# One more step between transposes and value products in a hybrid attention and S5 layer, with S5's scans in two steps and its rotation back on GpSimd

## The chip, the cores and the metric

The kernel runs on one core of a Trainium2 chip. The metric is the device time of one execution in microseconds; the median of three runs of the kernel before is 1433.84 us (1433.35 to 1434.98). Engines are named as the profile names them: PE (matmuls) and PEld (its weight loads), DVE (VectorE), ACT (ScalarE), POOL (GpSimd), SP (the engine that issues most DMAs).

## What is computed

One encoder layer over 2048 positions of 1024 channels, in float32. A projection is split into latent attention (4 heads) and an S5 branch (32 groups of 16 channels, 64 complex states, forward and backward); both branches are normed, gated, joined and projected back. Cut to what matters here:

```
for each block of queries and each head:                       # attention
    s = qn . k_nope + qr . k_rope                              # scores
    p = softmax(s * scale);   o = p . v
bu = einsum(u, b_bar)                                          # S5, both directions
_, h = associative_scan(h_t = lam_bar * h_(t-1) + bu_t)
y  = Re(einsum(h, c)) + d_skip * u
```

## The kernel before

The kernel writes out the order of every engine by hand: each engine executes its instructions in the order in which the code issues them (`manual_schedule`), and an instruction that waits holds up all that stand behind it on its engine. There are three stages. The first projects the input. The second, in which the change lies, is attention with S5 between its pieces. The third mixes, projects back and stores.

**The attention stage** is a loop over steps `t` (L1547). A unit is 256 queries of one head; there are 32 units of 8 steps, so 256 steps with scores. In step `t`:

- `scores` (L1098): five matmuls of 512 columns into a PSUM tile `sc` (two buffers), then DVE takes the negative maximum `nm` (L1108).
- `expo` (L1111): ACT writes `e = exp(sc + nm)` (L1114) into a ring of 13 tiles. Nine steps later `norm` scales it on ACT (L1143).
- `transp` (L1145), 11 steps after the exponential (`LAG`): four PE transposes of two `e` tiles into PSUM `pt` (two buffers); ACT rounds them to `phi` (L1159) and DVE stores the rest `plo = pt - phi` (L1573). Both have two buffers.
- `av` (L1163), `AVLAG` = 1 step after the transposes: six matmuls that read `phi` and `plo` (L1171 to L1173) and add into `av` in PSUM (one buffer). After a unit's eighth `av`, ACT copies the sum to `avs` (L1176), and one step later `unit_out` multiplies it by a weight into `po` (L1180), which ACT copies to `o` (L1182).
- Pieces of `qprep` (L703) make the queries of the next block of four units: 19 pieces, in the steps that a rule allows (steps 4 of a unit are left out, step 3 only ends a piece). They use the PSUM pool `psQ`, which has one buffer. `unit_out` uses the same buffer, in step 4 of a unit.

**S5 between them.** A group of channels (`group`, L950) starts every 7 steps (twice after 6), and takes 15 steps, so two groups are always under way. "pre" pieces stand ahead of a step's scores, "post" pieces behind its value products. Counted from the group's start: steps 0 to 3 make tables on POOL (`w`, `tmp`, `t`, `t3b`; L905 to L975), step 3 turns `w` on PE, step 5 makes `px` on PE, step 6 multiplies it by phasors on DVE (`ta`, `tb`, L996 and L997), step 7 adds them to `X` (L1001), step 8 scans them in four scans on DVE (L1008 and L1009, two for each of the real and imaginary parts, into `G`), step 9 turns them back (`hc` on DVE at L1017, `tb` on POOL at L1018), step 10 subtracts (L1021, DVE), and step 14 multiplies `hc` into `py` on PE (L1034). Other POOL work of the stage: tables `v` of the next four groups, splits `ul` and `ml`, and `qd` of the queries (L750).

The loop's end, as it matters here:

```
        # (without scores in between, its operands take a step longer)
        lag = AVLAG + (t >= 8 * NU)
        m, j = divmod(t - LAG - lag, 8)
        if 0 <= m < NU and t != 8 * NU:
            av(sts[m], j)
        m, j = divmod(t - LAG - lag - 1, 8)
        if 0 <= m < NU and j == 7:
            unit_out(*units[m], sts.pop(m))
        s5_post(t)
```

Of the kernel before, what the change touches and what calls it, by code (L numbers as in the profile page):

```python
# [21 lines left out]
P = 128  # L22
# [11 lines left out]
T = 8  # L34
# [22 lines left out]
class Metered:  # L57
    """An engine that counts the elements it is given."""
# [13 lines left out]
class Scratch:  # L72
    """Temporaries of one shape, out of a ring of tiles of 512 (or, if small, 32) elements."""
# [10 lines left out]
def reduce_angle(eng, sc, out, ang):  # L84
    """out = ang - 2 pi round(ang / 2 pi)."""
    k = sc()
    eng.tensor_scalar(k, ang, 1.0 / TWO_PI, MAGIC, ALU.mult, ALU.add)
    eng.tensor_scalar(k, k, MAGIC, None, ALU.subtract)
    yield
    eng.scalar_tensor_tensor(out, k, -PI_1, ang, ALU.mult, ALU.add)  # L90
    for c in (PI_2, PI_3, PI_4):
        yield
        eng.scalar_tensor_tensor(out, k, -c, out, ALU.mult, ALU.add)
    yield


def sincos(eng, sc, sin_out, cos_out, r):
    """sin and cos of r in about [-pi, pi], from those of r / 2."""
# [23 lines left out]
def exp_of(eng, sc, pool, out, x):  # L122
    """exp(x) in float32, exact at 0."""
# [24 lines left out]
def tile_hymba(ctx, tc, x, pos, inv_freq, pre_g, w_in, q_g, w_uqT, w_uqr, kv_g, w_ukT, w_uv, attn_g,  # L148
# [35 lines left out]
    def rsqrt_of(ss, n, scale, eps=EPS):  # L184
        """(ss * scale + eps) ** -0.5 on [128, n]."""
        v = sm.tile([P, n], F32, tag=f"rv{n}", name="rv")
        r = sm.tile([P, n], F32, tag=f"rr{n}", name="rr")
        V.tensor_scalar(v, ss, scale, eps, ALU.mult, ALU.add)
        G.tensor_tensor(r, v, nhalf[:, :n], ALU.pow)
        return r  # L190

    def split(hi, lo, src, scale=None):
        """hi + lo = src (* a scale for each partition), both float32r."""
        if scale is None:
            A.activation(hi, src, AF.Copy)
            V.tensor_tensor(lo, src, f32(hi), ALU.subtract)
        else:
            A.activation(hi, src, AF.Copy, scale=scale)
            V.scalar_tensor_tensor(lo, src, scale, f32(hi), ALU.mult, ALU.subtract)
# [6 lines left out]
    # tables of the attention phase; those of S5 go through DRAM, by groups  # L206
# [11 lines left out]
    # ------------------------------------------------------------------ phase 1  # L218
# [51 lines left out]
    def turn(xt, t):  # L270
        """The tile's transpose, split, as tile t of a pair."""
# [34 lines left out]
    def gemm_t(nm, half):  # L306
        """Two blocks of 128 columns of a pair of tiles, with the columns in the partitions."""
# [43 lines left out]
    def s5_params():  # L351
# [37 lines left out]
        # F = (lam_bar - 1) / lam  # L389
# [17 lines left out]
        # powers of lam_bar, 0 .. T, in the order of each direction  # L407
# [29 lines left out]
        # phasors of chunk 32 i + 2 j + a: ph32 * (0..7) (+ phi), for a = 0, 1, and ph2 * (0..15)  # L437
# [13 lines left out]
        for nm, src in (("b", ph2), ("a", ph32)):  # L451
# [21 lines left out]
            # the backward direction turns the other way  # L473
# [11 lines left out]
        # B_bar = F B; B'' = B_bar e^{-i phi}; C' = lam_bar C  # L485
# [3 lines left out]
        def cm(orr, oi, ar, ai, xr_, xi_):  # L489
            """(orr, oi) = (ar + i ai)(xr + i xi), a over the last dimension."""  # L490
# [32 lines left out]
        # centre lag: Re(C B_bar) of both directions + D  # L523
        # (eight groups at a time: theirs are the blocks on the diagonal)
# [36 lines left out]
    def step():  # L561
        """A slice of the tables, of about BUDGET elements."""
# [4 lines left out]
    def blocks(s):  # L567
        """The columns of two tiles, a block of columns at a time: z goes first and last, tile by tile,
        so that the next tiles can take the places of these meanwhile."""
# [8 lines left out]
    # absorbed weights: W_uq[h] W_uk[h]^T  # L578
# [23 lines left out]
    # the first tile is loaded and normed by halves  # L602
# [48 lines left out]
    # ------------------------------------------------------------------ phase 2  # L651
    # (the gate columns of the last two tiles run under its start)
# [5 lines left out]
    ep = pool(ph2, "ep", 13)  # L658
    pp = pool(ph2, "pp", 2)
# [36 lines left out]
    # queries of a block of 256: each piece's last results are split a step later  # L696
# [74 lines left out]
    def both(*gens):  # L771
        """Step some routines in turn; what each returns."""
# [14 lines left out]
    # the gate columns of the last two tiles run under the start of the attention  # L787
# [58 lines left out]
    # S5  # L846
# [8 lines left out]
    def s5_load(q):  # L855
        """The tables of four groups."""
# [34 lines left out]
    def ops4(tile_, q_r, q_i, c1, c2):  # L891
        """The operands of tile_[., 2, s, h] = q_r[s] c1[., h] + q_i[s] c2[., h]."""
# [9 lines left out]
    def two(eng, tile_, tmp, *o):  # L902
        """The two products of a table; later they are added."""
# [18 lines left out]
    def k_build(q):  # L922
        """The kernels of the lags within a chunk, and their windows for each position."""
# [26 lines left out]
    def group(g):  # L950
        """A group of channels, a step at a time: what is ready first, what needs the PE last."""
        q, i = divmod(g, 4)
        f = S5[q]
        # (chunks in the order of their tiles: those of the even, then those of the odd places)
# [9 lines left out]
        # phasors over the chunks: -sin, cos, sin  # L964
# [39 lines left out]
        # (the states that enter the chunks; nothing enters the first, or the last backwards)  # L1004
# [6 lines left out]
        yield "pre"  # L1011
        yield "post"
# [4 lines left out]
        V.tensor_tensor(of_tiles(hc), g4, co, ALU.mult)  # L1017
# [3 lines left out]
        V.tensor_tensor(hc, hc, tb2, ALU.subtract)  # L1021
        yield "pre"
        yield "post"
# [20 lines left out]
    # when each group starts; the tables of the next four groups are made meanwhile  # L1044
# [52 lines left out]
    # attention  # L1097
# [19 lines left out]
    # the blocks of a row were shifted by their own maxima: bring them to the row's, and divide  # L1117
# [45 lines left out]
    def av(st, j):  # L1163
# [10 lines left out]
        if j == 7:  # L1174
            st["avs"] = op.tile([P, 256], F32, tag="avs", name="avs")
# [9 lines left out]
    # ------------------------------------------------------------------ weights of phase 3  # L1185
# [52 lines left out]
    # ------------------------------------------------------------------ phase 3  # L1238
    # (pairs of tiles, with the channels in the partitions up to W_out)
    def mixer():  # L1240
# [26 lines left out]
        def gelu(d):  # L1267
            """y <- 2 gelu(y), and its parts"""
# [38 lines left out]
        def part(d, src, h, c):  # L1307
            """hi and lo of half h of src, as blocks c .. of the products' operands"""
# [16 lines left out]
        def summed(d, sq):  # L1325
            """The sums of squares of the four channels in a partition"""
# [5 lines left out]
        def attn(d):  # L1332
            """o gated, and its parts"""
# [16 lines left out]
        def ssm(d):  # L1350
            """y <- 4 y sigmoid(. + b), gated into g, and its parts"""
# [37 lines left out]
        # the columns of the result in the parts that are worked on; the last tile ends in smaller ones  # L1389
# [11 lines left out]
        def comb(d, t, cs):  # L1401
            """Both branches by their factors, summed; the mean of the squares; times the gain"""
# [40 lines left out]
        # the first pairs, in small steps between those of the attention  # L1443
# [98 lines left out]
    NLAG, LAG, AVLAG = 9, 11, 1  # L1542
# [4 lines left out]
    for t in range(8 * NU + LAG + AVLAG + 3):  # L1547
        n, i = divmod(t, 8)
        # what the step before has made ready
# [5 lines left out]
        # scores  # L1555
# [23 lines left out]
        # (without scores in between, its operands take a step longer)  # L1579
        lag = AVLAG + (t >= 8 * NU)  # L1580
        m, j = divmod(t - LAG - lag, 8)
        if 0 <= m < NU and t != 8 * NU:
            av(sts[m], j)
        m, j = divmod(t - LAG - lag - 1, 8)
# [3 lines left out]
        # the queries of the next block  # L1588
# [37 lines left out]
def layout(i):  # L1626
    """The inputs, laid out for the core; nothing is computed from them."""
# [51 lines left out]
```

## Time and profile before

| | before |
|---|---|
| time, median of 3 runs | 1433.84 us (1433.35 to 1434.98) |
| span of the profiled execution | 1431.5 us |
| PE busy | 1359.6 us, 95% |
| PEld busy | 1221.6 us, 85% |
| DVE busy | 1053.7 us, 74% |
| ACT busy | 789.0 us, 55% |
| POOL busy | 624.9 us, 44% |

The span runs from the first to the last instruction of the one profiled execution; the time of the runs holds 2.3 us more. PE's busy time counts matmuls whose ends are modelled, so a busy PE is not PE at its peak. The 256 steps of the attention stage lie between about 394 and 1168 us of the span.

### The profile page before, as it was taken

How to read it: one execution, taken by the hardware profiler on the slowest of the kernel's cores; microseconds unless marked ns; L12 is line 12 of the kernel's file. 1: busy time of each engine (PE TensorE's matmuls, PEld its weight loads, DVE VectorE, ACT ScalarE, POOL GpSimd, SP SyncE). 2: the span in 40 equal slices, each digit the busy share in tenths (PEclk: the TensorE clock that was granted, in tenths of full speed). 3: DMA queues.
4: the chain of work that ended last, by engine and by line, in shares of the span. 5: the costliest groups of instructions: out<-in, count | busy, mean ns of one | idle time of the engine just before them, and what ended most of it. 6: DMA issues, size and time to landing. Idle time of an engine off the chain costs nothing.

```text
span 1431.5 us, 24291 instructions
## 1 busy us (share of the span) xinstructions
PE 1359.6 (95%) x9016; PEld 1221.6 (85%) x9016; DVE 1053.7 (74%) x1876; ACT 789.0 (55%) x1796; POOL 624.9 (44%) x616
## 2 busy tenths in 40 slices
PE   7999999999989999999999998999999989999998
PEld 7999999999968788887888887887888878788886
DVE  5456545332588888898989888988888895876774
ACT  6321222122457767767677676676677775544542
POOL 2102321233364655555556555645542695323340
PEclk9999999999999999999999999999999999999999
DMA  8322332442610110201102011020100345345432
GB/s 293 89 61 66 80 87 73 98 122 73 150 35 19 39 34 5 54 19 31 41 5 61 12 32 41 23 43 5 32 5 9 101 128 131 118 148 179 145 103 88
DMA packets 122133, 102.91 MB, mean 72 GB/s; under 512 B 14672, under 2 KB 107104, under 8 KB 122016
## 3 DMA queue, kind: packets, MB, share of 16 engines
q1 hardware_dynamic: 110384, 89.43, 22.3%
q0 software_dynamic: 2272, 7.62, 2.0%
q10 hardware_dynamic: 9360, 4.33, 1.5%
q8 instruction: 70, 1.15, 0.3%
q14 instruction: 47, 0.39, 0.1%
HBM read 63.80 MB, written 37.54 MB: 71 GB/s over the span
## 4 chain that ended last, share of the span: by engine, by line
PE 59%; DVE 26%; ACT 5%; issue 4%; POOL 2%; DMA 2%; SPq 1%; ACTq 0%; POOLq 0%; DVEq 0%
DVE plo L1573 5%; DVE nm L1108 4%; PE po L202 4%; PE po L203 4%; PE po L204 4%; PE pt L1151 3%; DVE hc L1017 3%; DVE G L1009 3%; DVE G L1008 3%; PE z_ga L203 2%; PE z_ga L204 2%; PE z_ga L202 2%; PE av L1173 2%; PE z_u L204 2%; PE z_u L202 2%
## 5 line engine op out<-in xcount | busy, mean ns | idle before, releaser
L1114 ACT ACTIVATE e<-sc,nm 128x512 f32<-128x512 f32 x256 | 176.4, 689 | 141.1 <-DVE nm L1108 139.8
L1573 DVE TENSOR_TENSOR plo<-pt,phi 128x512 fp32r<-128x512 f32 x255 | 175.0, 686 | 49.2 <-ACT phi L1159 46.3
L1159 ACT ACTIVATE phi<-pt 128x512 fp32r<-128x512 f32 x256 | 152.8, 597 | 72.9 <-PE pt L1151 72.4
L1108 DVE TENSOR_REDUCE nm<-sc 128x1 f32<-128x512 f32 x256 | 175.0, 683 | 17.6 <-PE sc L1107 15.6
L1173 PE MATMUL av<-plo,kn_h 128*128 128x256 f32 x512 | 150.6, 294 | 30.0 <-DVE plo L1573 29.5
L1171 PE MATMUL av<-phi,kn_h 128*128 128x256 f32 x512 | 165.7, 324 | 13.3 <-ACT avs L1176 13.2
L1143 ACT ACTIVATE e<-e,f 128x512 f32<-128x512 f32 x226 | 163.8, 725 | 1.5 <-DVE f L1132 1.5
L1151 PEld LDWEIGHTS pt<-ident,e 128*128 128x128 f32 x1024 | 127.8, 141 | 38.9 <-DVE e L1139 4.5
L1151 PE MATMUL pt<-ident,e 128*128 128x128 f32 x1024 | 154.8, 274 | 4.3 <-DVE e L1139 3.5
L1172 PE MATMUL av<-phi,kn_l 128*128 128x256 f32 x512 | 144.6, 282 | 0.0
L1173 PEld LDWEIGHTS av<-plo,kn_h 128*128 128x128 f32 x512 | 96.5, 189 | 40.1 <-DVE plo L1573 39.3
L1018 POOL TENSOR_TENSOR tb<-G,t 128x512 f32<-128x512 f32 x32 | 41.6, 1301 | 192.2 <-DVE G L1009 192.2
L1103 PE MATMUL sc<-kT_h,qo 128*128 128x512 f32 x256 | 114.7, 448 | 2.9 <-ACT e L1114 1.4
L1171 PEld LDWEIGHTS av<-phi,kn_h 128*128 128x128 f32 x512 | 97.6, 191 | 16.6 <-ACT avs L1176 16.5
L202 PE MATMUL po<-woh,ah 128*128 128x512 f32 (+1 forms) x264 | 102.6, 389 | 1.9 <-ACT u L1410 1.9
L203 PE MATMUL po<-wol,ah 128*128 128x512 f32 (+1 forms) x264 | 102.4, 388 | 0.0
L204 PE MATMUL po<-woh,al 128*128 128x512 f32 (+1 forms) x264 | 102.3, 388 | 0.0
L1104 PE MATMUL sc<-kT_l,qo 128*128 128x512 f32 x256 | 101.5, 396 | 0.0
L1106 PE MATMUL sc<-krS,qo 128*128 128x512 f32 x256 | 101.3, 396 | 0.0
L1107 PE MATMUL sc<-krS,qo 128*128 128x512 f32 x256 | 101.2, 395 | 0.0
L1105 PE MATMUL sc<-kT_h,qo 128*128 128x512 f32 x256 | 100.8, 394 | 0.0
L1172 PEld LDWEIGHTS av<-phi,kn_l 128*128 128x128 f32 x512 | 97.7, 191 | 0.0
(337 smaller groups left out, 4148.6 us busy)
## 6 DMA issues: line engine op xcount, KB each, us to landing
g_d<-gst SPq DMA_DIRECT2D x64, 128.0 KB, 2.0
g<-g_d SPq DMA_DIRECT2D x16, 512.0 KB, 5.7
xr<-in_x_dram SPq DMA_DIRECT2D x16, 512.0 KB, 6.7
xt<-in_x_dram SPq DMA_DIRECT2D x15, 512.0 KB, 3.8
out_dram<-res SPq DMA_DIRECT2D x15, 512.0 KB, 3.1
u_d<-ust ACTq DMA_DIRECT2D x64, 64.0 KB, 2.1
u<-u_d SPq DMA_DIRECT2D x64, 64.0 KB, 2.5
o_d<-o SPq DMA_DIRECT2D x32, 128.0 KB, 1.8
```

What stands on the lines that cost most here:

```text
L202: PE.matmul(ps, ahi, bhi, start=first, stop=False)
L203: PE.matmul(ps, ahi, blo, start=False, stop=False)
L204: PE.matmul(ps, alo, bhi, start=False, stop=last)
L1108: V.tensor_reduce(st["nm"][:, qt, kb:kb + 1], ps, AX.X, ALU.max, negate=True)
L1114: A.activation(e, st.pop("s"), AF.Exp, bias=st["nm"][:, qt, kb:kb + 1], accum_out=st["L"][:, qt, kb:kb + 1])
L1143: A.activation(e, e, AF.Copy, scale=f)
L1151: PE.transpose(pt[:, kk, qt, :], st["e"][qt, kt // 4][:, o:o + P], ident)
L1159: A.activation(hi, ptf, AF.Copy)
L1171: PE.matmul(o, kn_h[:, kt, :], hi[:, w], start=kt == 0, stop=False)
L1172: PE.matmul(o, kn_l[:, kt, :], hi[:, w], start=False, stop=False)
L1173: PE.matmul(o, kn_h[:, kt, :], lo[:, w], start=False, stop=kt == NT - 1)
L1573: V.tensor_tensor(lo[0], lo[1], f32(lo[2]), ALU.subtract)
```

## The change

The value products follow two steps behind the transposes (`AVLAG` 1 to 2), `phi` and `plo` get three buffers, the ring of `e` goes from 13 tiles to 12 and `avs` from two to one. The lag behind the last scores was two steps before and still is, so the special case there goes. S5's four scans are spread over two steps, the real part's two in step 8 and the imaginary part's two in step 9. The rotation back moves a step, to 10 and 11, and its DVE product (L1017) and its subtraction (L1021) go to POOL. `py` stays in step 14. Comments are blanked too, and lines below the loop's special case stand two to four lines higher.

```diff
-    ep = pool(ph2, "ep", 13)
-    pp = pool(ph2, "pp", 2)
+    ep = pool(ph2, "ep", 12)
+    pp = pool(ph2, "pp", 3)
...
         for r in range(2):
             o = r * NC
             V.tensor_tensor_scan(gt[0:64, o + 2:o + NC + 1], df[0:64], xm[0:64, r, 0:NC - 1], 0.0, ALU.mult, ALU.add)
             V.tensor_tensor_scan(gt[64:P, o + 1:o + NC][:, ::-1], df[64:P], xm[64:P, r, 1:][:, ::-1], 0.0,
                                  ALU.mult, ALU.add)
-        yield "pre"
-        yield "post"
+            yield "pre"
+            yield "post"
...
-        V.tensor_tensor(of_tiles(hc), g4, co, ALU.mult)
+        G.tensor_tensor(of_tiles(hc), g4, co, ALU.mult)
         G.tensor_tensor(of_tiles(tb2), g4[:, ::-1], si, ALU.mult)
         yield "pre"
         yield "post"
-        V.tensor_tensor(hc, hc, tb2, ALU.subtract)
-        yield "pre"
-        yield "post"
+        G.tensor_tensor(hc, hc, tb2, ALU.subtract)
...
-            st["avs"] = op.tile([P, 256], F32, tag="avs", name="avs")
+            st["avs"] = op.tile([P, 256], F32, tag="avs", name="avs", bufs=1)
...
-    NLAG, LAG, AVLAG = 9, 11, 1
+    NLAG, LAG, AVLAG = 9, 11, 2
...
-    for t in range(8 * NU + LAG + AVLAG + 3):
+    for t in range(8 * NU + LAG + AVLAG + 2):
...
-        lag = AVLAG + (t >= 8 * NU)
-        m, j = divmod(t - LAG - lag, 8)
-        if 0 <= m < NU and t != 8 * NU:
+        m, j = divmod(t - LAG - AVLAG, 8)
+        if 0 <= m < NU:
             av(sts[m], j)
-        m, j = divmod(t - LAG - lag - 1, 8)
+        m, j = divmod(t - LAG - AVLAG - 1, 8)
```

The built order of the instructions shows three places. The first is DVE's queue where a group is scanned and turned back. `nm` and `plo` are the attention's two DVE instructions of a step, and the scans print as SCALAR_TENSOR_TENSOR. Before:

```order
L1008 SCALAR_TENSOR_TENSOR G_4637<-tab_6803,X_4639 64x255
L1009 SCALAR_TENSOR_TENSOR G_4637<-tab_6803,X_4639 64x255
L1008 SCALAR_TENSOR_TENSOR G_4637<-tab_6803,X_4639 64x255
L1009 SCALAR_TENSOR_TENSOR G_4637<-tab_6803,X_4639 64x255
L1108 TENSOR_REDUCE nm<-sc 128x1
L1573 TENSOR_TENSOR plo<-pt_8811,phi 128x512
L1017 TENSOR_TENSOR hc<-G_4637,t_8563 128x512
L1108 TENSOR_REDUCE nm<-sc 128x1
L1573 TENSOR_TENSOR plo<-pt_8853,phi 128x512
L732 SCALAR_TENSOR_TENSOR qo_1_8828<-psq,kvgs,qo_1_8828 128x256
L1021 TENSOR_TENSOR hc<-hc,tb_8839 128x512
```

The same group in the changed kernel:

```order
L1008 SCALAR_TENSOR_TENSOR G_4637<-tab_6797,X_4639 64x255
L1009 SCALAR_TENSOR_TENSOR G_4637<-tab_6797,X_4639 64x255
L1106 TENSOR_REDUCE nm<-sc 128x1
L1571 TENSOR_TENSOR plo<-pt_8797,phi 128x512
L1008 SCALAR_TENSOR_TENSOR G_4637<-tab_6797,X_4639 64x255
L1009 SCALAR_TENSOR_TENSOR G_4637<-tab_6797,X_4639 64x255
L1106 TENSOR_REDUCE nm<-sc 128x1
L1571 TENSOR_TENSOR plo<-pt_8843,phi 128x512
L732 SCALAR_TENSOR_TENSOR qo_1_8820<-psq,kvgs,qo_1_8820 128x256
L1106 TENSOR_REDUCE nm<-sc 128x1
```

Two scans stand between one step's `plo` and the next step's `nm`, where four stood, and the two `hc` instructions are gone from DVE.

The second place is POOL's queue from one group's turn back to the next group's tables (`t`, `t3b`: phasor tables of the next group; `w`, `v`: tables of later ones; `G` are the scanned states). Before:

```order
L1018 TENSOR_TENSOR tb_8036<-G_4638,t_7745 128x512
L971 TENSOR_TENSOR t_8039<-tab_6803 128x768
L972 TENSOR_TENSOR t3b<-tab_6803 128x768
L975 TENSOR_TENSOR t_8039<-t_8039,t3b 128x768
L905 TENSOR_TENSOR v<-tab_7930 128x256
L906 TENSOR_TENSOR tmp<-tab_7930 128x256
L915 TENSOR_TENSOR v<-v,tmp 128x256
```

In the changed kernel:

```order
L971 TENSOR_TENSOR t_8029<-tab_6797 128x768
L972 TENSOR_TENSOR t3b<-tab_6797 128x768
L1017 TENSOR_TENSOR hc<-G_4638,t_7735 128x512
L1018 TENSOR_TENSOR tb_8059<-G_4638,t_7735 128x512
L975 TENSOR_TENSOR t_8029<-t_8029,t3b 128x768
L1021 TENSOR_TENSOR hc<-hc,tb_8059 128x512
L905 TENSOR_TENSOR v<-tab_7924 128x256
L906 TENSOR_TENSOR tmp<-tab_7924 128x256
L915 TENSOR_TENSOR v<-v,tmp 128x256
```

POOL now waits for the scans behind the next group's `t` and `t3b`, not ahead of them, and carries two more instructions of 512 elements in each group.

The third place is PE's queue around `unit_out` (`po`) and a piece of the queries (`ptr`, four transposes of `qd`), which both write the one buffer of `psQ`. Before, `po` stands a step earlier, at the end of the step of `pt_6544`, and the queries' piece at the end of this one:

```order
L1151 MATMUL pt_6583<-ident,e 128x128 x4
L1171 MATMUL av<-phi,kn_h 128x256
L1172 MATMUL av<-phi,kn_l 128x256
L1173 MATMUL av<-plo,kn_h 128x256
L1171 MATMUL av<-phi,kn_h 128x256
L1172 MATMUL av<-phi,kn_l 128x256
L1173 MATMUL av<-plo,kn_h 128x256
L758 MATMUL ptr_6600<-ident,qd 128x128 x4
L1103 MATMUL sc<-kT_h,qo_2_5050 128x512
```

In the changed kernel:

```order
L1149 MATMUL pt_6569<-ident,e 128x128 x4
L1169 MATMUL av<-phi,kn_h 128x256
L1170 MATMUL av<-phi,kn_l 128x256
L1171 MATMUL av<-plo,kn_h 128x256
L1169 MATMUL av<-phi,kn_h 128x256
L1170 MATMUL av<-phi,kn_l 128x256
L1171 MATMUL av<-plo,kn_h 128x256
L1178 MATMUL po<-avs,wuv 128x256
L758 MATMUL ptr_6592<-ident,qd 128x128 x4
L1101 MATMUL sc<-kT_h,qo_2_5044 128x512
```

`po` has moved from step 4 of a unit to step 5, in which the queries' rule lets a piece begin: the piece follows it in the same step. In the whole order a piece of the queries follows `po` in its step 17 times, before never; six of these have S5 matmuls between the two (three times `py` from `hc`, three times `py` and `px`).

## Rows read from the trace of the kernel before

**Rows 1.** The page's part 1: busy us, share of the span, instructions.

```profile
PE 1359.6 (95%) x9016; PEld 1221.6 (85%) x9016; DVE 1053.7 (74%) x1876; ACT 789.0 (55%) x1796; POOL 624.9 (44%) x616
```

**Rows 2.** Busy time by stage; columns: stretch, us, five engines, granted clock, DMA share, GB/s.

```profile
0.00:394.20 394.20, 383.81 (x2929) 374.41 (x2929) 193.89 (x460) 117.99 (x256) 93.39 (x130) 1.00 0.40 108
394.20:1167.90 773.70, 725.30 (x4713) 632.86 (x4714) 679.84 (x1163) 543.66 (x1273) 429.87 (x400) 1.00 0.14 33
1167.90:1431.50 263.60, 250.49 (x1377) 214.29 (x1375) 179.93 (x256) 127.34 (x268) 101.63 (x87) 0.99 0.43 131
```

**Rows 3.** Waits of PE in 394.2 to 1167.9: us in total, times, longest.

```profile
PE av L1173 <- DVE plo L1573: 29.1, 34, 2.6
PE av L1171 <- ACT avs L1176: 12.8, 11, 1.8
```

**Rows 4.** Waits of PE's weight loads in the same stretch, same columns.

```profile
PEld av L1173 <- DVE plo L1573: 38.7, 44, 2.8
PEld av L1171 <- ACT avs L1176: 15.8, 13, 2.0
```

**Rows 5.** The chain that ended last, around one step: start us, us, what.

```profile
739.60 0.23 PE sc L1103
...
740.76 0.44 PE pt L1151 x4
...
741.90 0.12 PE py L202
...
742.25 0.12 PE px L202
...
742.97 0.23 PE sc L1103
```

**Rows 6.** Groups of DVE in the stage: busy us, mean ns, then idle before them.

```profile
L1108 DVE TENSOR_REDUCE nm<-sc 128x1 f32<-128x512 f32 x255 | 174.3, 683 | 17.6 <-PE sc L1107 15.6
L1573 DVE TENSOR_TENSOR plo<-pt,phi 128x512 fp32r<-128x512 f32 x243 | 166.8, 686 | 45.1 <-ACT phi L1159 42.1
L1017 DVE TENSOR_TENSOR hc<-G,t 128x512 f32<-128x512 f32 x32 | 52.3, 1635 | 0.0
L1009 DVE TENSOR_TENSOR_SCAN G<-tab,X 64x255 f32<-64x255 f32 x64 | 46.3, 724 | 0.9
...
L1021 DVE TENSOR_TENSOR hc<-hc,tb 128x512 f32<-128x512 f32 x32 | 41.3, 1292 | 2.5 <-POOL tb L1018 2.5
L1001 DVE TENSOR_TENSOR X<-ta,tb 128x512 f32<-128x512 f32 x32 | 23.8, 743 | 0.0
```

**Rows 7.** DVE in order of time behind one group's scans: start us, us.

```profile
730.03 0.69 DVE L1573 TENSOR_TENSOR plo<-pt,phi 128x512 fp32r<-128x512 f32 x1
730.63 2.02 DVE L1017 TENSOR_TENSOR hc<-G,t 128x512 f32<-128x512 f32 x1
```

**Rows 8.** POOL in the same stretch.

```profile
729.35 1.30 POOL L1018 TENSOR_TENSOR tb<-G,t 128x512 f32<-128x512 f32 x1 [4.59 <-DVE G L1009]
730.61 1.50 POOL L971 TENSOR_TENSOR t<-tab 128x768 f32<-128x768 f32 x1
```

**Rows 9.** Groups of POOL in the stage: busy us, mean ns, idle before.

```profile
L975 POOL TENSOR_TENSOR t<-t,t3b 128x768 f32<-128x768 f32 x32 | 63.1, 1971 | 2.2
...
L1018 POOL TENSOR_TENSOR tb<-G,t 128x512 f32<-128x512 f32 x32 | 41.6, 1301 | 192.2 <-DVE G L1009 192.2
```

**Rows 10.** All engines around one `unit_out`, in order of time.

```profile
701.70 0.59 PE L1180 MATMUL po<-avs,wuv 128*128 128x256 f32 x2
...
701.94 0.58 PE L1103 MATMUL sc<-kT_h,qo 128*128 128x512 f32 x1
...
702.40 0.39 ACT L1182 ACTIVATE o<-po 128x256 f32<-128x256 f32 x1
...
704.44 1.03 PE L1034 MATMUL py<-hc,v 128*128 128x256 f32 x4
...
705.12 0.47 PE L202 MATMUL psr<-wqr_h,zh 128*128 128x256 f32 x1
```

## The prediction

> **What bounds the kernel now.** I read the busy times first, then the same by stage, then the waits of PE and of its weight loads, then the chain of waits around single steps, and last the groups and the order in time of the engines that PE waits for. PE is busy 95% of the span [rows 1], but that is an average of three stages. In the first stage PE misses 10 us of 394 and in the third 13 of 264; in the attention stage it misses 48 of 774, at the full granted clock, 1.00, the level of 2.4 GHz [rows 2]. The change touches only that stage, so what it can give is what PE loses there.
>
> The waits name the loss. PE stands idle 29.1 us before products that read `plo`, which DVE makes, and 12.8 us before the first product of a unit, which needs the `avs` copy of the unit before to be done [rows 3]. The weight loads, which run ahead of the matmuls and so show a stop earlier, wait 38.7 and 15.8 us for the same two [rows 4]. The reader is to see that both views put nearly all of the loss on these two places: 41.9 us by the matmuls, whose modelled ends cover the beginning of each wait, and 54.5 us by the loads. I take 54.5 us as what can be won at most from waits that are named.
>
> That it is a loss and not work shows in a step without a wait. In the chain the five score matmuls start at 739.60, the transposes at 740.76, and after the products S5's matmuls at 741.90: 2.30 us for the attention's part. S5's nine matmuls take it to 742.97, 1.07 us more [rows 5]. The stage has 255 steps from the first scores to the last in 773.7 us [rows 2], so 3.03 us a step on average; without 54.5 us of waits it would be 2.82 us.
>
> DVE is why `plo` is late. It is busy 679.84 us of the stage [rows 2], 2.67 us a step, against a PE that could run at 2.82; that is near enough to fall behind wherever the work is bunched. `hc` and its subtraction take 1635 and 1292 ns on average, while `X`, an addition of the same size from SBUF to SBUF, takes 743 and `plo` 686 [rows 6]. The order in time shows why: `hc` begins at 730.63, as POOL begins `t` at 730.61, and ends at 732.65, 0.54 us after POOL's instruction has [rows 7, 8]. So an instruction of DVE with both operands in SBUF stands still while POOL runs one, and `plo`, one operand of which is in PSUM, does not: 0.69 us at 730.03, while POOL runs from 729.35 to 730.65. In a group four scans of 724 ns [rows 6], and one step later the long `hc` and the long subtraction, all stand ahead of some step's `plo`; PE can't pass, since its next products read it.
>
> **The change part by part.**
>
> *The products a step later.* `plo` may be one step late, 2.8 us, before PE waits for it. The longest wait of PE for `plo` is 2.8 us, and 38.7 us over 44 waits is 0.9 us each [rows 4], so the slack alone covers nearly all of them. But it removes no work from DVE, and PE then runs into the next limits: scores need an `sc` buffer that the exponential of two steps before has freed, which needs that step's `nm` from the same DVE. Alone, I would expect a good part of 38.7 us to come back at `sc`. The three buffers of `phi` and `plo` keep a step's ACT and DVE work from waiting for products two steps back. The shorter ring of `e` costs nothing: tile `t - 12` was last read by the transposes of step `t` or earlier, and ACT's `phi` of step `t`, which stands ahead of the exponential, waits for these anyway. One `avs` is enough, since it is read a step after it is written and rewritten eight steps later.
>
> *DVE without `hc`.* 52.3 + 41.3 = 93.6 us leave DVE [rows 6]: 586 us remain, 2.30 us a step against PE's 2.82. This cures the cause, and is hidden by nothing: it is what makes `nm` come in time, for `sc` and for `avs` too, whose copy stands on ACT behind an exponential that waits for `nm`.
>
> *The scans in two steps.* A scan step held 2.8 us of scans and 1.4 us of `nm` and `plo`, above any step of PE's; now two steps hold 1.4 + 1.4 = 2.8 us each, which is about PE's step. The heaviest DVE steps are now even.
>
> *POOL with `hc`.* The product should cost what its twin `tb` costs, 1301 ns. For the subtraction I have the addition of 768 elements, 1971 ns, so 1.31 us for 512, between 1.30 and 1.97 as bounds [rows 9]. 32 x 2.61 = 84 us more: POOL goes from 429.87 [rows 2] to 514 us in a stage of some 735, 70%. What hides it is POOL's idle time, 192.2 us of which are spent waiting for the scans [rows 9]. The result is needed in step 14 and is begun in step 10: POOL has four steps, 11 us, for `hc`, `tb`, the `t` addition and the subtraction, 1.3 + 1.3 + 2.0 + 1.3 = 5.9 us. If that cover is gone, PE waits for `hc` at `py`. The next group's `t` and `t3b` come out of the wait for the scans, which is easier for them.
>
> *DVE against POOL.* The instructions that still read SBUF twice on DVE are `X`, the scans and the small ones of the row statistics. They stand late in the 7 steps, when POOL has mostly gone through its queue. POOL's load becomes 514/32 = 16 us of a group's 20 (7 x 2.82), so `X` will meet it at times. A meeting costs what `hc` paid, 2.02 - 0.68 = 1.34 us with `plo` for the bare cost [rows 7]. I take one meeting a group, 1.34 x 32 = 43 us of DVE, which DVE has: 629 us, 2.47 a step. The Trainium skill says of this in SBUF — State Buffer, "Who interferes with whom", that only DVE's and GpSimd's shared ports contend, and that whoever holds them holds them for a whole instruction. The trace agrees (2.02 us beside 0.69). By that rule each of the five instructions of a group would meet POOL as often as POOL is busy, 0.7, and wait half a meeting, 0.67 us: 75 us of DVE in the stage in place of 43. DVE would then hold 661 us, 2.59 a step, still under PE's, and the sum stays.
>
> *The new meeting in `psQ`.* `po` now stands in step 5 of a unit, in which a queries' piece may follow at once; both want the one buffer, and the rule still keeps step 4 free. 17 times the piece must wait until ACT has copied `po`. Before, PE had issued `po` by 701.94 and ACT's copy ended at 702.79: 0.85 us [rows 10]. Eleven bare cases cost 9.4 us; three with `py` between (704.44 to 705.12, 0.68 us [rows 10]) 0.5 us; three with nine matmuls (1.07 us [rows 5]) nothing. 9.9 us together, and between nothing (PE late anyway) and 17 x 1.7 = 29 (a copy that a late exponential holds up as long again).
>
> **The sum.** 54.5 us of named waits, less 9.9 for `psQ`, 4 that stay of the wait for `plo` (a tenth), and 5 of the wait for `avs` (a third: one buffer of `av` remains, and the copy still stands behind an exponential) gives 35.6. The profiled execution had a span of 1431.5 us and the runs' median lies 2.3 above it, so 1395.9 + 2.3, about 1398 us.
>
> **Rivals.**
>
> *The wait moves.* PE runs into `sc` and into ACT. ACT is busy 543.66 us of the stage [rows 2], 2.13 a step, and works in order; a short PE step of 2.30 us leaves it little room. Then `avs` keeps all of its 15.8, the `plo` waits come back by half as waits for the exponential, 19, and `psQ` takes 9.9: 54.5 - 44.7 = 10 us won, 1424. For it: after the change no engine between PE and PSUM has gained a buffer but `phi`. Against: DVE's 93.6 us are gone, and the present waits of PE for the exponential are small enough not to be among the first two.
>
> *POOL holds DVE.* This ends on the other side. If POOL's queue has not run out when the next group's `X` and scans come, each of the five waits 1.34 us: 6.7 us a group, where the removed two cost 2.9. DVE then has 586/32 = 18.3 + 6.7 = 25.0 us a group, against 773.7/32 = 24.2 now (the stage's last steps counted in): 0.8 x 32 = 26 us slower, 1460. It decides from 5.9 us a group, more than four of the five held. For it: POOL's load of 16 us nearly fills the time from the second pair of scans to the next first pair, 20 - 2.8 - 1.4 = 15.8. Against: the load counts work that is spread, such as `qd` and the weights at the end. The Trainium skill speaks for it in Perfetto Trace Analysis, "Optimizing Scalar/DVE Operations": since the two engines share a port of SBUF, moving work from the one to the other might not help. The trace agrees so far as `hc` paid 1635 ns.
>
> *It does nothing.* If the waits in the trace were only PE's spare time before another limit, all 54.5 us would come back, 1434. Against: the limit would have to be PE itself, and PE does a step in 2.30.
>
> **Chances.** My forecast 0.80, the moved wait 0.12, POOL holding DVE 0.05, nothing 0.03. The predicted time is the likeliest, 1398. Its own range runs from 1379 (all 54.5 us won and `psQ` free) to 1417 (`psQ` at 29 us); the range given, 1380 to 1420, reaches toward the moved wait and leaves out the far part of it. A measurement of this kernel tells 0.2%, 3 us, from no change: faster 0.91, within 0.2% 0.03, slower 0.06.
>
> **What the profile after would show.** The wait of the products for `plo` gone, and DVE's busy time in the stage near 590 to 630 us. `hc` and the subtraction on POOL at about 1.3 us each. Scans and `X` still near 0.7 us; above 1.2 us the second rival is at work. A new wait of PE's query matmuls for ACT's `o`, some 10 us. If the named waits of PE for the exponential or `avs` grow above 20 us, the first rival holds. The first and third stages should keep their 394 and 264 us. The prediction is wrong if POOL sits idle little and `py` waits for it, or if PE's short steps turn out to be paced by ACT.

## The result and the profile after

The changed kernel takes 1411.2 us (median of 4 runs, 1410.1 to 1413.6), the kernel before 1433.6 beside it: ratio 0.9844, 95% interval 0.983 to 0.9858. It is 22.4 us faster; 35.6 were forecast. 1411 lies inside the range given, 1380 to 1420, but in its slower half.

The stages of the changed kernel, with the columns of [rows 2]:

```profile
0.00:393.70 393.70, 384.38 (x2929) 374.91 (x2929) 193.54 (x460) 117.69 (x256) 93.35 (x130) 1.00 0.40 109
393.70:1143.20 749.50, 715.82 (x4707) 626.93 (x4708) 620.80 (x1099) 546.40 (x1273) 497.82 (x464) 1.00 0.14 34
1143.20:1408.30 265.10, 252.84 (x1383) 216.25 (x1382) 179.71 (x255) 127.01 (x268) 101.09 (x87) 0.99 0.43 130
```

The attention stage is 24.2 us shorter, 749.5 for 773.7, and the third stage 1.5 us longer. DVE's busy time in the stage fell by 59 us and POOL's rose by 68. The waits of PE's weight loads in the stage, which answer to [rows 4]:

```profile
PEld sc L1101 <- ACT e L1112: 16.6, 19, 2.7
PEld ptr L758 <- ACT o L1180: 8.1, 5, 3.1
PEld av L1169 <- ACT avs L1174: 7.8, 10, 1.8
PEld psq L202 <- ACT o L1180: 6.3, 4, 2.6
PEld psr L202 <- ACT o L1180: 1.9, 2, 0.9
```

In the kernel before, the score matmuls waited for the exponential as well, a little:

```profile
PEld sc L1103 <- ACT e L1114: 3.6, 6, 1.2
```

The wait for `plo` is gone and that for `avs` halved. In their place stand 16.6 us of score matmuls that wait for the exponential, and 16.3 us in three rows of queries' matmuls that wait for ACT's `o`: the meeting in `psQ`. These named waits come to 40.7 us; before, the waits for `plo`, for `avs` and of the scores came to 58.1.

DVE's groups in the stage, as in [rows 6], and POOL's two new ones, as in [rows 9]:

```profile
L1009 DVE TENSOR_TENSOR_SCAN G<-tab,X 64x255 f32<-64x255 f32 x64 | 57.1, 892 | 0.9
L1008 DVE TENSOR_TENSOR_SCAN G<-tab,X 64x255 f32<-64x255 f32 x64 | 51.8, 810 | 0.0
L1001 DVE TENSOR_TENSOR X<-ta,tb 128x512 f32<-128x512 f32 x32 | 30.8, 963 | 0.0
...
L1017 POOL TENSOR_TENSOR hc<-G,t 128x512 f32<-128x512 f32 x32 | 41.6, 1300 | 134.8 <-DVE G L1009 106.4 <-PE pt L1149 12.3 <-PE av L1171 10.7
L1021 POOL TENSOR_TENSOR hc<-hc,tb 128x512 f32<-128x512 f32 x32 | 41.4, 1292 | 0.6
```

`hc` and the subtraction cost on POOL what was forecast, 83 us. POOL's other instructions took 15 us less than before; that DVE's two had held them in their turn would fit, and is not tested. The scan of L1009 has gone from 724 to 892 ns and `X` from 743 to 963: they are now the ones that POOL holds. One group's scans and `X` on DVE show it:

```profile
860.93 1.98 DVE L1001 TENSOR_TENSOR X<-ta,tb 128x512 f32<-128x512 f32 x1
...
864.83 2.16 DVE L1009 TENSOR_TENSOR_SCAN G<-tab,X 64x255 f32<-64x255 f32 x1
```

POOL in the same stretch:

```profile
860.87 1.50 POOL L971 TENSOR_TENSOR t<-tab 128x768 f32<-128x768 f32 x1
862.32 1.95 POOL L972 TENSOR_TENSOR t3b<-tab 128x768 f32<-128x768 f32 x1
864.35 2.09 POOL L975 TENSOR_TENSOR t<-t,t3b 128x768 f32<-128x768 f32 x1
```

`X` began 0.06 us after `t` and ended at 862.91, 0.54 us behind it; the scan ended at 866.99, 0.55 us behind the addition. POOL is held in its turn: `t3b` began at 862.32, while `X` was still at work, and took 1.95 us where `t`, of the same size, took 1.50. What holds the scans and `X` are mostly the tables of the next group, which in the kernel before POOL reached only after these scans: in the trace of the stage, 22 of the 31 us by which scans and `X` exceed their undisturbed time (139.7 us for 108.7) fall on instructions that met `t`, `t3b` or their addition.

The longest meeting in `psQ`, PE, ACT and the DMA that ACT waited for, in order of time:

```profile
838.03 0.59 PE L1178 MATMUL po<-avs,wuv 128*128 128x256 f32 x2
839.24 0.63 ACT L887 ACTIVATE mh<-m 128x512 fp32r<-128x512 f32 x1 [2.66 <-DMA m<-k_d]
839.78 0.58 ACT L1157 ACTIVATE phi<-pt 128x512 fp32r<-128x512 f32 x1
...
840.25 0.68 ACT L1112 ACTIVATE e<-sc,nm 128x512 f32<-128x512 f32 x1
...
840.92 0.38 ACT L1180 ACTIVATE o<-po 128x256 f32<-128x256 f32 x1
...
841.35 0.65 PE L758 MATMUL ptr<-ident,qd 128*128 128x128 f32 x4 [2.73 <-ACT o L1180]
```

`po` was on its way at 838.03 and its copy came at 840.92, since `phi`, the exponential and, here, a split that waited for its DMA stand ahead of it on ACT. All of PE's later work stood behind the four transposes of the queries until 841.35.

### The profile page after: what moved, and what is told of

Its sections match the earlier page's. It is cut to its first block, busy times and chain, and to the rows that moved or that the text cites. A ratio compares the mean times of both kernels' runs of the same rounds, so it can differ in the third digit from the quotient of the medians.

```text
span 1408.3 us, 24276 instructions
## 1 busy us (share of the span) xinstructions
PE 1353.0 (96%) x9016; PEld 1218.1 (86%) x9016; DVE 994.0 (71%) x1812; ACT 791.1 (56%) x1796; POOL 692.3 (49%) x680
## 4 chain that ended last, share of the span: by engine, by line
PE 70%; DVE 16%; ACT 6%; issue 3%; POOL 2%; DMA 1%; SPq 1%; POOLq 0%; ACTq 0%; DVEq 0%
PE pt L1149 5%; PE po L202 4%; PE po L204 4%; PE po L203 4%; DVE nm L1106 3%; PE sc L1101 3%; DVE G L1009 2%; PE sc L1102 2%; PE sc L1105 2%; PE sc L1104 2%; PE sc L1103 2%; PE av L1169 2%; PE av L1170 2%; PE av L1171 2%; PE z_ga L203 2%
## 5 line engine op out<-in xcount | busy, mean ns | idle before, releaser
L1106 DVE TENSOR_REDUCE nm<-sc 128x1 f32<-128x512 f32 x256 | 175.4, 685 | 45.5 <-PE sc L1105 42.7
L1171 PE MATMUL av<-plo,kn_h 128*128 128x256 f32 x512 | 144.4, 282 | 0.4 <-DVE plo L1571 0.4
L1017 POOL TENSOR_TENSOR hc<-G,t 128x512 f32<-128x512 f32 x32 | 41.6, 1300 | 134.8 <-DVE G L1009 106.4
L189 POOL TENSOR_TENSOR rr<-rv,nhalf 128x1 f32<-128x1 f32 (+1 forms) x23 | 17.0, 741 | 163.7 <-DVE rv L188 163.7
```

What stands on the lines that cost most here:

```text
L1106: V.tensor_reduce(st["nm"][:, qt, kb:kb + 1], ps, AX.X, ALU.max, negate=True)
L1171: PE.matmul(o, kn_h[:, kt, :], lo[:, w], start=False, stop=kt == NT - 1)
```

## The experiments

Each was timed against the kernel before on the same chip. "The moved rule" below is the edit of the third.

**The two halves of the change, and its S5 half by parts.** `e1_lag_only` takes only the attention's part of the diff:

```diff
-    NLAG, LAG, AVLAG = 9, 11, 1
+    NLAG, LAG, AVLAG = 9, 11, 2
```

with the buffers and the loop's end as in the change.

> Only the attention part of the change: products two steps behind the transposes, three buffers of both parts, 12 tiles of e, one avs; S5 as before, with hc and its subtraction on DVE. Theory (DVE's lateness is the cause, the lag only moves the wait): the wait of the products for plo goes, 38.7 us by the weight loads, and most of it comes back as waits of the score matmuls for the exponential and of the first products for avs, 25 us or more together; psQ adds its meeting; time 1420 to 1432 us. Rival (the lag is the gain, DVE's work was only in the way of plo): waits for the exponential stay under 10 us and the time is about that of the changed kernel, 1405 to 1415 us.

Measured: 1453.2 us, ratio 1.0137 (1.0114 to 1.0161), slower than either theory had it. The weight loads' waits:

```profile
PEld sc L1103 <- ACT e L1114: 31.3, 35, 3.1
PEld av L1171 <- ACT avs L1176: 21.1, 17, 2.5
PEld ptr L758 <- ACT o L1182: 8.9, 5, 2.3
PEld psq L202 <- ACT o L1182: 7.5, 4, 2.5
PEld psr L202 <- ACT o L1182: 3.7, 4, 1.4
```

The wait for `plo` is gone. In its place stand 31.3 us at the scores, where 3.6 stood, and 5.3 more at `avs`; 20.1 us of `psQ` come on top. There is a price that I had not counted, the clock. Eight stretches of 2 us of this run, columns as in [rows 2]:

```profile
622.00:624.00 2.00, 1.67 (x13) 1.34 (x12) 2.00 (x4) 1.45 (x4) 1.92 (x2) 1.00 0.00 0
624.00:626.00 2.00, 1.25 (x8) 0.83 (x6) 2.00 (x2) 0.43 (x1) 1.94 (x3) 1.00 0.00 0
626.00:628.00 2.00, 0.52 (x4) 0.52 (x5) 1.21 (x3) 1.62 (x5) 1.84 (x4) 1.00 0.00 0
628.00:630.00 2.00, 1.38 (x7) 0.66 (x6) 1.45 (x3) 1.84 (x5) 1.92 (x4) 0.59 0.03 8
630.00:632.00 2.00, 2.00 (x8) 1.90 (x9) 0.00 (x0) 0.42 (x2) 0.28 (x1) 0.50 0.23 66
632.00:634.00 2.00, 2.00 (x7) 1.51 (x7) 0.28 (x1) 0.66 (x2) 0.00 (x0) 0.50 0.00 0
634.00:636.00 2.00, 2.00 (x14) 2.00 (x13) 1.15 (x3) 1.37 (x4) 0.00 (x0) 0.70 0.00 0
636.00:638.00 2.00, 2.00 (x15) 1.74 (x14) 1.58 (x4) 0.51 (x1) 0.00 (x0) 1.00 0.00 0
```

PE, the first of the five busy times, falls to 0.52 us of 2, and the granted clock then goes to 0.50, the level of 1.2 GHz, while PE is fully busy; it is back at 1.00 in the last row. Over the whole run the granted clock is 0.991, against 0.997 before: by an estimate from these two, 0.006 x 1447 = 9 us. The attention stage of this execution is 16.1 us longer than before (789.8 for 773.7): PE is idle 9.8 us more and busy 6.3 us more (731.6 for 725.3). Slower matmuls would show in the second of these, so the estimate looks somewhat high.

`e2_s5_only` is the other half, S5's part of the diff on the kernel before, with the lag of one.

> Only the S5 part of the change: scans in two steps, rotation back on GpSimd; products one step behind the transposes as before, two buffers, 13 tiles of e. Theory (DVE's 93.6 us are the cause): the wait for plo falls from 38.7 us by the weight loads to under 20 without any lag, there is no meeting in psQ, and the time is 1408 to 1420 us. Rival (the lag is the gain): plo keeps over 30 us of waits and the time stays above 1425 us.

Measured: 1402.5 us, ratio 0.9787 (0.9772 to 0.9801), below the theory's range, though `plo` keeps 22.3 us of waits, a little more than it said. The rival falls, and the half is faster than the whole.

`e11_hc_pool_only` takes only two lines of it:

```diff
-        V.tensor_tensor(of_tiles(hc), g4, co, ALU.mult)
+        G.tensor_tensor(of_tiles(hc), g4, co, ALU.mult)
...
-        V.tensor_tensor(hc, hc, tb2, ALU.subtract)
+        G.tensor_tensor(hc, hc, tb2, ALU.subtract)
```

> The kernel before with nothing changed but the engine of hc and its subtraction, GpSimd in place of DVE: lag of one, scans in one step, rotation in steps 9 and 10. Theory (this move alone is the gain): 1398 to 1408 us, with waits for plo of 15 to 28 us by the weight loads. Rival (without spreading or lag the four scans ahead of a step's plo keep PE waiting): 1415 us or more.

Measured: 1400.2 us, ratio 0.9766 (0.9751 to 0.9781). The weight loads' waits for what PE waited for before:

```profile
PEld av L1173 <- DVE plo L1573: 18.4, 26, 2.9
PEld av L1171 <- ACT avs L1176: 5.4, 7, 1.7
```

So 33 us come from two instructions moved to another engine, with no lag and no spreading: the wait for `plo` halves and that for `avs` falls to a third. The intervals of this kernel and of the S5 half overlap: spreading the scans with the rotation a step later, as the change does it, gave nothing.

`e5_hc_dve` is the opposite, the changed kernel with those two lines back on DVE.

> The changed kernel with the rotation back on VectorE again (hc and its subtraction), in its new steps 10 and 11; scans still in two steps, products still two steps behind. Theory (it is hc and the subtraction on DVE, held by GpSimd, that make DVE late): DVE's busy time in the stage rises from 621 to 670 us or more, waits for the exponential and avs rise by 10 us or more, and the time is 1418 to 1428 us. Rival (the bunch of four scans was the cause, and spreading them is enough): the time stays within 4 us of the changed kernel's 1411.

Measured: 1443.5 us, ratio 1.0078 (1.0058 to 1.0098), 16 us above the theory's range: waits for the exponential 24.5, for `avs` 21.7 and for `o` 20.3 us, and a granted clock of 0.990. The rival falls: the two lines are worth 32 us in the changed kernel too.

**The meeting in `psQ`.** `e3_rule` is the changed kernel with the queries' rule moved on by a step, as `po` was:

```diff
-            if qb and (held if i == 3 else i != 4 and PLACE.get(t, (0, 0))[1] in QOFF):
+            if qb and (held if i == 4 else i != 5 and PLACE.get(t, (0, 0))[1] in QOFF):
```

> The changed kernel with the queries' rule moved on by a step, as po has moved: step 5 of a unit is left out in place of step 4, and step 4 only ends a piece in place of step 3, so no piece follows po in its step. Theory (the meeting in psQ costs what the waits for ACT's o show, 11.8 us by the matmuls and 16.3 by the weight loads): those waits go and the time falls by 9 to 16 us, to 1395 to 1402 us. Rival (while PE waits for o, DVE and ACT catch up, so the waits come back at the scores): the time falls by under 4 us, and the waits of the scores for the exponential rise from 16.6 us to over 25.

Measured: 1397.4 us, ratio 0.9747 (0.9732 to 0.9761), 13.8 us under the changed kernel. The waits for `o` are down to 0.6 us, and what is left is:

```profile
PEld sc L1101 <- ACT e L1112: 12.6, 19, 2.5
PEld av L1169 <- ACT avs L1174: 11.0, 13, 2.3
```

The rise at `avs`, 3 us, is all that came back; the theory holds. Against `e2_s5_only`, which lacks only the lag, its buffers and the moved rule, this kernel is 5 us faster.

`e6_lag_rule` is the kernel of `e1_lag_only` with the moved rule.

> The kernel before with the lag of two and its buffers, and with the queries' rule moved on by a step so that no piece follows po; S5 as before. Theory (the lag by itself gives next to nothing while DVE is late, and the 20 us by which the lag alone was slower are the meeting in psQ, 20.1 us of waits by the weight loads, with the clock dips that follow it): time 1428 to 1438 us, as the kernel before. Rival (the lag itself is harmful, since PE runs ahead into the one buffer of av and the two of sc): 1442 us or more. Second rival (the lag is a gain once psQ is free): 1422 us or less.

Measured: 1429.2 us, ratio 0.9969 (0.9958 to 0.9981). With `psQ` free the lag alone gives 4 us and no more: 28.3 us of waits for the exponential and 19.5 for `avs` stand where 38.7 for `plo` and 15.8 for `avs` stood. The theory holds; the meeting turned a small gain into a loss of 20 us.

**The scans and the order of POOL's queue.** `e7_rule_one_scan` has the moved rule, and all scans in step 8 with the rotation on POOL in steps 9 and 10, the places of the kernel before.

> The changed kernel with the moved queries' rule, and S5's four scans in one step again; hc and its subtraction stay on GpSimd, one step earlier, py where it is. Theory (what counts is the amount of work on DVE and GpSimd's holding of it, not the bunching): within 4 us of the 1397 us of the same kernel with scans in two steps. Rival (the spreading of the scans is a large part of the gain): 1403 us or more, with waits of the scores for the exponential 8 us or more above the 12.6 us there.

Measured: 1394.0 us, ratio 0.9716 (0.97 to 0.9732), the fastest kernel of the study, with 13.7 us of waits for the exponential: the theory holds, bunching the scans again costs nothing here. It differs from `e11_hc_pool_only` in the lag, its buffers and the moved rule alone, and the intervals of the two lie apart (0.97 to 0.9732, 0.9751 to 0.9781): with DVE relieved and `psQ` free, the lag is worth 6 us. `e10_rule_one_scan_hc_late` differs from `e7_rule_one_scan` in one thing: the rotation stands a step later, in 10 and 11, as the change has it.

```diff
+        yield "pre"
+        yield "post"
         g3 = gt[:, 1:2 * NC + 1].rearrange("p (a c) -> p a c", a=2)
...
         G.tensor_tensor(hc, hc, tb2, ALU.subtract)
-        yield "pre"
-        yield "post"
```

> The changed kernel with the moved queries' rule, all four scans in step 8, and the rotation back in steps 10 and 11 as in the changed kernel, so that GpSimd's queue has the next group's t and t3b ahead of its wait for the scans. Theory (in the changed kernel the order of GpSimd's queue sets t and t3b against the scans on DVE, and what spreading the scans gives is given back by that): scans and X are held by 20 us or more in all, as with the scans in two steps (32 us) and unlike the 9 us with the rotation in steps 9 and 10, and the time is 1397 to 1406 us. Rival (GpSimd's order does not matter, the scans are simply better bunched): 1391 to 1396 us, as with the rotation in steps 9 and 10.

Measured: 1419.1 us, ratio 0.9898 (0.988 to 0.9916): 25 us slower than the kernel that it differs from by this step, more than the theory said. DVE's scans and `X` in `e7_rule_one_scan`:

```profile
L1009 DVE TENSOR_TENSOR_SCAN G<-tab,X 64x255 f32<-64x255 f32 x64 | 47.1, 736 | 0.9
L1008 DVE TENSOR_TENSOR_SCAN G<-tab,X 64x255 f32<-64x255 f32 x64 | 46.1, 721 | 0.4
L1001 DVE TENSOR_TENSOR X<-ta,tb 128x512 f32<-128x512 f32 x32 | 24.1, 752 | 0.0
```

and in `e10_rule_one_scan_hc_late`:

```profile
L1009 DVE TENSOR_TENSOR_SCAN G<-tab,X 64x255 f32<-64x255 f32 x64 | 60.7, 948 | 0.9
L1008 DVE TENSOR_TENSOR_SCAN G<-tab,X 64x255 f32<-64x255 f32 x64 | 56.0, 874 | 0.4
L1001 DVE TENSOR_TENSOR X<-ta,tb 128x512 f32<-128x512 f32 x32 | 28.1, 880 | 0.0
```

The later wait lets POOL run the next group's `t` and `t3b` against the scans, and the scans and `X` are held 27.5 us more. In the traces 29 us of this kernel's holding fall on instructions that met `t`, `t3b` or their addition, and 1 us of that of `e7_rule_one_scan`. The waits of the scores for the exponential are 29.0 us for 13.7, and the granted clock is 0.991 for 0.998, 10 us of 1420.

`e13_spread_forward` spreads the scans the other way, without that step: the first two behind `X` in step 7, the others in step 8, the rotation in 9 and 10.

> The changed kernel with the moved queries' rule and the scans spread the other way: the real part's two in step 7 behind X, the imaginary part's two in step 8, and the rotation on GpSimd in steps 9 and 10, so that GpSimd waits for the scans ahead of the next group's t and t3b, as in the kernel before. Theory (spreading the scans helps, and in the changed kernel GpSimd's order gave it back): X and the scans are held under 12 us in all, and the time is 1380 to 1391 us, under the 1394 us of the scans in one step with the same order. Rival (with GpSimd's order kept, bunched scans cost nothing more): 1392 us or more.

Measured: 1395.1 us, ratio 0.974 (0.9724 to 0.9756). It is no faster than the bunched scans with the same order: the rival holds. The scans and `X` are held 15 us, a little more than the theory said. By these three and the changed kernel with the moved rule, spreading is worth 22 us where POOL runs against the scans (1419 to 1397), and nothing where it doesn't (1394 to 1395). Read the other way, POOL's order costs 25 us with bunched scans and only 2 with spread ones, although the scans and `X` take about as long in both kernels with the later wait (144.8 and 141.0 us). So holding DVE costs much where four scans stand in one step, and little where they are spread.

`e9_rule_pool_more` adds to the changed kernel with the moved rule two subtractions on POOL in each group, whose results nothing reads:

```diff
         G.tensor_tensor(hc, hc, tb2, ALU.subtract)
+        for _ in range(2):
+            G.tensor_tensor(tb2, hc, tb2, ALU.subtract)
```

> The changed kernel with the moved queries' rule, and with two more subtractions of 512 elements on GpSimd in each group, whose results nothing reads: 2.6 us more in a group of 20. Theory (DVE has slack, so GpSimd's holding it costs little until its queue no longer runs out before the next scans): scans and X are held 20 us more in all, and the time rises by 3 to 12 us, to 1400 to 1409. Rival (GpSimd's holding of DVE is already what the remaining waits come from): the time rises by 15 us or more.

Measured: 1410.6 us, ratio 0.9839 (0.982 to 0.9859), 13 us more, between the two theories. POOL is busy 593.85 us of a stage of 750.8. The scans and `X` are held only 8.4 us more (149.4 for 141.0), not the 20 of the theory; the scores wait 17.5 us for the exponential, for 12.6, and one `py` waits 3.6 us for POOL's split `ml`, for 1.0. So more work on POOL costs before its queue is full. How the 13 us divide between POOL's holding of DVE and its own lateness is not shown.

**Two attempts to use the lag further.** `e8_rule_plo_late` has DVE write a step's `plo` behind the next step's maximum:

```diff
             scores(qo[b][h], sts[n], i)
+            if pend is not None:
+                V.tensor_tensor(pend[0], pend[1], f32(pend[2]), ALU.subtract)
+                pend = None
...
-        if lo is not None:
+        if lo is not None and t < 8 * NU - 1:
+            pend = lo
+        elif lo is not None:
             V.tensor_tensor(lo[0], lo[1], f32(lo[2]), ALU.subtract)
```

> The changed kernel with the moved queries' rule, and with plo of a step written by DVE behind the next step's maximum in place of behind its own, which the lag of two allows. Theory (DVE idles before plo until ACT has made phi, 57 us in the stage of the changed kernel, and stands late for the next maximum because of it): DVE's wait for phi goes to under 15 us, the waits of the scores for the exponential fall below 8 us, and the time is 1386 to 1394 us. Rival (what remains of PE's waits comes from ACT's own queue, not from a late maximum): within 3 us of 1397.

Measured: 1410.1 us, ratio 0.9833 (0.9817 to 0.9848), 13 us slower than without the edit. Two of the three forecasts of the theory came true, no wait for `phi` among DVE's first five and 2.9 us for the exponential, and the time went the other way:

```profile
PEld pt L1149 <- issue: 24.6, 17, 3.1
PEld pt L1149 <- PE sc L1105: 20.1, 26, 1.2
PE pt L1149 <- DVE plo L1561: 26.1, 27, 2.7
```

The weight loads of the transposes, which waited 1.9 us without the edit, now wait 44.7 us. Their rows don't name the cause, but the row of the matmuls does: 26.1 us of waits for `plo`. A `plo` that comes a step later frees `pt`'s two buffers a step later. Whether a third buffer would turn this into a gain was not tested.

`e12_s5_behind_nm` moves `s5_pre(t)` behind `transp` in the kernel of `e7_rule_one_scan`, so that S5's instructions stand between the maximum and `plo`.

> The kernel with the lag of two, the moved queries' rule, the rotation on GpSimd and the scans in one step (1394 us), with S5's first pieces of a step issued behind the step's scores and transposes in place of ahead of them: on DVE they stand between the maximum and plo, where DVE idles 69 us for ACT's phi, and the maximum no longer waits for them; plo has the lag's slack. Theory (what is left of PE's waits is a late maximum, by way of the exponential): the waits of the scores and of av for ACT fall from 19 us by the weight loads to under 8 and the time is 1378 to 1389 us. Rival (plo, now behind the scans, keeps the two buffers of pt and the transposes wait as much): 1391 us or more.

Measured: 1415.3 us, ratio 0.9874 (0.9858 to 0.989), 21 us slower. The time is in the rival's range, but its mechanism is small: `pt` waits 4.8 us for `plo`. The waits of the scores and `av` for ACT did not fall, 21.7 us for 18.2. ACT's own waits for DVE have moved:

```profile
ACT e L1114 <- DVE nm L1108: 76.9, 57, 3.4
ACT f L1125 <- DVE f L1124: 18.7, 17, 3.1
```

In `e7_rule_one_scan` they were:

```profile
ACT e L1114 <- DVE nm L1108: 96.4, 78, 3.1
ACT f L1125 <- DVE f L1124: 2.3, 4, 0.7
```

The maximum comes earlier, but the row statistics (`f`) still stand behind S5's work on DVE, and ACT waits there instead: 95.6 us for the two together, for 98.7. The granted clock fell from 0.998 to 0.993; how the 21 us divide stays open.

## Why the prediction was right, and where it was off

- *DVE's lateness is the cause.* Right, and more than was said: the two lines alone give 33 us, which is more than the whole change gives. DVE's busy time of 620.8 us lies in the 590 to 630 forecast, and the meetings with POOL cost 31 us of DVE (139.7 us of scans and `X` in the stage, less 108.7 at their undisturbed 0.67 to 0.69) against 43 taken. The reason given for few meetings failed, though: that `X` and the scans stand late, "when POOL has mostly gone through its queue". In the trace POOL runs the next group's `t` beside `X`. So did the sign that scans and `X` are "still near 0.7 us": they took 0.81 to 0.96, and 43 us over five instructions would have made 0.95.
- *The products a step later.* The prediction said that alone a good part of the wait would come back at `sc`. That was so, and yet the sum left nothing for it: it had 4 us for `plo` and 5 for `avs`, and the run has none and 7.8, with 16.6 us at the scores. This is the first rival in part, below the 20 us that were to be its sign, and the larger of the sum's two mis-sized terms.
- *The meeting in `psQ`.* The mechanism was right, 9.9 us too small: 13.8 by the run without it. The trace has the 17 meetings. In four of the eleven bare ones ACT was in time, and the queries' first matmul starts 0.92 us behind `po`'s last one, which fits the price of 0.85; in the other seven it starts 1.10 to 3.11 us behind it.
- *The scans in two steps.* Wrong as a gain of the change. Two sentences failed: that the evenly spread scans help, and that the next group's `t` and `t3b` "come out of the wait for the scans, which is easier for them". That is where they began to hold the scans. The two cancel, 22 us against 25, and the sum had a term for neither: that it did not miss by more is luck.
- *POOL holds DVE.* The second rival did not decide the sign, but its mechanism does not wait for four held instructions of five: where the scans are bunched, 27.5 us more of holding go with 25 us of time. The rule of the Trainium skill in SBUF — State Buffer, "Who interferes with whom", that whoever issues first keeps the shared ports for its whole instruction, agrees with every held instruction of DVE shown here: POOL's had begun first, and DVE's ended 0.54 or 0.55 us behind it. The warning in its Perfetto Trace Analysis, "Optimizing Scalar/DVE Operations", that offloading between the two might not help, did not apply here: `e11_hc_pool_only` is 2.3% faster.
- *The sum.* The named waits fell by 17.4 us (58.1 to 40.7), while the stage lost 24.2. The matmuls' own rows account for it: PE's idle time fell by 14.7 us (48.4 to 33.7) and its busy time by 9.5 (725.30 to 715.82). The largest piece of the second is the product that reads `plo`, whose matmuls took 6.8 us less once they no longer started behind a wait:

```profile
L1173 PE MATMUL av<-plo,kn_h 128*128 128x256 f32 x486 | 143.2, 295 | 29.6 <-DVE plo L1573 29.1
L1171 PE MATMUL av<-plo,kn_h 128*128 128x256 f32 x484 | 136.4, 282 | 0.0
```

- *The parts.* By the runs, the two lines give 33 us, the spreading with the later rotation gives nothing (2 us slower, `e2_s5_only`), and the lag as made costs 9 (1411 for 1402): its meeting in `psQ` costs 14, and the lag itself gives 5. Both errors of the sum go the same way. Without the meeting the change gives 36 us (`e3_rule`), where the sum had 45.5 (54.5 less 4 and 5), and the meeting cost 14 in place of 9.9.

## What to carry to other kernels

When an instruction moves to another engine, read that engine's queue from the new wait on: what the wait used to hold back will now run, and against whom. When a lag changes, move every rule that was set by the old step with it; here a single buffer shared by two steps that meet cost 14 us, where the lag gave 5. A lag without relief for the late engine only moves the wait to the next buffer.

## What the hardware showed that was not expected

- Bunched waits of PE can cost twice. In `e1_lag_only`, after PE had been busy 0.52 us of 2, the granted clock went to 0.50 and stayed there for about 5 us in which PE was fully busy again. The four executions of that kernel took 1449.0 to 1456.9 us at mean clocks of 0.991 to 0.986. Across the kernels the picture is less clean: 0.990 and 0.991 at 1443, 1453 and 1419 us and 0.998 at 1394 and 1400, but 0.997 in the kernel before, at 1434.
- GpSimd holds VectorE's scans too, a scan of 0.69 us taking 2.16, and not only additions and products of two operands in SBUF. By these runs, what the holding costs depends on whether the scans are bunched: 17 us more of it cost 2 us with the scans spread (`e3_rule` against `e13_spread_forward`), and 27.5 us more cost 25 with all four in one step.
